# Softmax statistics of the head groups in token order over DRAM, and their factors broadcast by DMA

## The chip, the cores and the metric

The kernel runs on one core of a Trainium2 chip. The engines named here are TensorE (PE, its weight loads PEld), VectorE (DVE), ScalarE (ACT), GpSimd (POOL) and SyncE (SP), whose queue issues nearly all of the kernel's DMAs. The metric is the device time of one execution in microseconds (us), median of several runs.

## The reference

One step of a hybrid decoder layer for a prompt of 1024 tokens and 8 sampled tokens (1032 columns), model width 1024, all in fp32. What matters for the change is the attention branch:

- 3 head groups of 4 heads of 64, with windows and dilations (128, 1), (512, 4) and (2048, 16). Every token attends to itself and 128 earlier tokens at its group's dilation; each group gives an output `o` and a log-sum-exp `lse` for each token and head.
- The groups are combined per head slot:

```
w = softmax(stack(lses, axis=0), axis=0)
out[b,t,h,d] = sum over g of w[g,b,t,h] * o[g,b,t,h,d]
```

- The result (4 x 64 wide) goes through `w_attn_out`. Beside it stands a convolution branch (GLU, causal depthwise convolution of width 31, LayerNorm over the 1024 channels, swish, a projection). Both are weighted by sigmoid gates, summed and projected; then come a SwiGLU FFN and a gated per-layer embedding.

The kernel keeps for each group, token and head the negated maximum of the scores (`nm`) and the sum of exponentials (`l`). With m the smallest `nm` over the groups, a group's factor is f = exp(-(nm - m)) / sum over groups of exp(-(nm - m)) * l, and the combined output is the sum of f * o over the groups, `o` not yet divided.

## The kernel before

Activations lie with channels on the partitions and tokens along the free dimension, in three chunks of 384, 384 and 264 columns (`CH`). Every fp32 product is made of three matmuls of rounded halves (`mm3`, L256 to L258: high by high, high weight by low input, low weight by high input). A weight of 128 outputs is loaded as `raw` (512 KB) and split into `wh` by ScalarE and `wl` by VectorE. L116 is the helper through which every VectorE, ScalarE, GpSimd and SyncE instruction is recorded, so these are told apart by the names of their tiles.

The program runs in stages. Up to about 480 us it makes the convolution's input and the q, k, v projections, with the attention in units (class `Unit`) put between their banks. Then come the gate GEMMs: 8 weights into `d_gB` and 8 into `d_gA`, each over the three chunks. A chunk of one weight is a *bank*: 8 times `mm3`, 24 matmuls into one PSUM bank. The three banks of a weight are called a round here. At the end of a bank ScalarE makes the sigmoid `sg`, SyncE stores it, and `pump` lets the background work in `bg` issue a little (2.95 us by the planner's own count). The background is a list of generators, taken in order; each `yield` hands back. In this stage it holds the rest of the convolution and the sample tokens' attention, then `combine()` and then `layer_norm()`. After the gates comes the phase of `w_attn_out` on `oh` and `ol` (called the A phase here), whose first matmul is `g<-oh`, then the convolution's projection, the output projection, the FFN and the embedding.

The order of the instructions on an engine is settled when the program is built, by a scheduler that works on that issue order. Each engine then executes its own queue in that order: a waiting instruction holds all behind it, and SP's queue holds all DMAs behind a store that waits for its sigmoid.

`combine()` begins with the statistics in `NMs[g]` and `Ls[g]`, [128, 32] with a group's own order of query rows on the partitions. Masks (`mk`) and 16-row matmuls (L857) bring the first group, transposes (L861) the other two, to tiles `st` of 16 x 256, rows (head, token mod 4). There VectorE and ScalarE make the factors (`cM`, `Dn`); they are split into a high and a low part (`fx`, `fl`, the latter moved beside the former by a DMA). For each head pair `hp` the three groups' outputs come from DRAM as `ogl` (512 KB each), and L909 multiplies a constant selection matrix `sel` by `fx`, which spreads the factors over the partitions: 24 matmuls into PSUM. VectorE multiplies `ogl` by them and adds up the groups, in pieces of 128 x 512 whose tokens lie 4 apart (steps of 16 bytes): 12 multiplies and 8 additions. The result is split into `oh` and `ol`.

`layer_norm()` centres each chunk (`centre`: the mean by L1079 from `ysum`, then for each of 8 channel tiles `y - m` on VectorE, its square on ScalarE and a running sum `acc` on VectorE; L304 transposes the sum) and then scales it (`scale`: L316 spreads the reciprocal root, and each channel tile takes two scalar_tensor_tensor operations on VectorE and a sigmoid on ScalarE).

Of the kernel before, what the change touches and what calls it, by code (L numbers as in the profile page):

```python
# [41 lines left out]
CLASSIC = 3  # L42
NPG = 4
# [11 lines left out]
def decoder_step(ctx: ExitStack, tc: tile.TileContext, ins, outs):  # L55
# [87 lines left out]
    d_o = scratch("d_o", (3, 2, P, S))  # L143
    d_row = scratch("d_row", (4, SLOT))
# [15 lines left out]
    NMs = [const.tile([P, 32], F32, name=f"nm{g}") for g in range(3)]  # L160
    Ls = [const.tile([P, 32], F32, name=f"l{g}") for g in range(3)]
    osm = const.tile([P, 2, NS], F32, name="osm")
    cc = const.tile([P, 44], F32, name="cc")
# [400 lines left out]
    def stat_col(g, blk, head):  # L564
        if g == 0:
            return blk * 4 + head
        if g == 1:
            return (blk % 2) * 16 + head * 4 + blk // 2
        return (blk // 4) * 16 + head * 4 + blk % 4

    class Unit:
# [19 lines left out]
        def qk(self):  # L591
# [11 lines left out]
            for i, half in enumerate(self.halves):  # L603
                self.e[i] = e = sc("E")
                for blk in half:
                    o, nk = cols[blk]
                    for h in range(2):
                        head = hp * 2 + h
                        col = stat_col(g, blk, head)
                        if g < 2:  # L610
                            bv = biases[g][:, (head + 1) * 256 - nk:(head + 1) * 256]
                        else:
# [4 lines left out]
                                               scale=-1.0, scalar=3e38, accum_out=NMs[g][:, col:col + 1])  # L617
                        A.activation(ev, ev, AF.Exp, scale=-1.0, bias=NMs[g][:, col:col + 1],
                                     accum_out=Ls[g][:, col:col + 1])
# [16 lines left out]
        def pv(self):  # L636
# [20 lines left out]
            if self.last:  # L657
                SY.dma_start(d_o[g, self.hp], oT[:, :S])

# [92 lines left out]
    def sample_attention():  # L752
# [75 lines left out]
        selbt = cc[:, 36:44]  # L828
        for hp in range(2):
            TE.matmul(ps[:, hp * 8:hp * 8 + 8], acc[:, hp * P:(hp + 1) * P], selbt, start=True, stop=True)  # L830
            TE.matmul(ps[:, 16 + hp * 8:24 + hp * 8], acc[:, 512 + hp * P:512 + (hp + 1) * P], selbt,
                      start=True, stop=True)
# [5 lines left out]
    def combine():  # L838

        self32 = act("sel32")  # L840
        G.memset(self32[:, :1024], 0.0)
        for o in (0, 32):
            SY.dma_start(self32[o:o + 16, :1024], ins["sel16"])
        sel = act("sel", F32R)
        A.activation(sel[:, :1024], self32[:, :1024], AF.Copy)
        stt = []
        for which, src in ((0, NMs), (1, Ls)):
            per = []
            for g in range(3):
                ps = misc()  # L850
                if g == 0:
                    mk = sc("mk")
                    mkv = mk[:, :128].rearrange("p (a r) -> p a r", r=4)
                    V.tensor_mul(mkv, src[0].rearrange("p (a o) -> p a o", o=1).to_broadcast([P, 32, 4]),
                                 cc[:, 0:4].rearrange("p (o r) -> p o r", o=1).to_broadcast([P, 32, 4]))
                    for blk in range(8):
                        TE.matmul(ps[:16, blk * 32:(blk + 1) * 32], mk[:, blk * 16:(blk + 1) * 16], cc[:, 4:36],  # L857
                                  start=True, stop=True)
                else:
                    for e in range(2):  # L860
                        TE.transpose(ps[:16, e * P:(e + 1) * P], src[g][:, e * 16:(e + 1) * 16], ident)  # L861
                d = sc("st", (16, 256))
                if g < 2:
                    V.tensor_copy(d, ps[:16, :256])
                else:
                    V.tensor_copy(d.rearrange("p (l a) -> p l a", a=4),
                                  ps[:16, :256].rearrange("p (a l) -> p l a", a=4))
                per.append(d)
                yield
# [687 lines left out]
def _constants():  # L1557
# [10 lines left out]
    for hp in range(2):  # L1568
        for r in range(4):
            for f in range(P):  # L1570
                sel[(hp * 2 + f // 64) * 4 + r, hp * 4 + r, f] = 1.0
# [70 lines left out]
```

## Time and profile before

| | |
|---|---|
| time, median of 3 runs (range) | 1711.09 us (1710.15 to 1711.93) |
| profiled execution: its own time; its span | 1711.9 us; 1710.1 us |
| TensorE busy in the span | 1687.7 us (99%) |
| VectorE busy in the span | 1217.9 us (71%) |
| ScalarE; GpSimd busy | 618.0 us; 23.0 us |
| mean DMA traffic | 100 GB/s |
| convolution done on VectorE, `ysum` complete | about 555.2 us |
| first matmul of combine (L857) | 562.87 us |
| L909 matmuls | 583.0 to 601.7 us |
| first matmul of the A phase | 670.97 us |

Times of instructions are microseconds from the start of the span. A group's row gives the line, the engine, the operation, output and inputs with their shapes, the count, the busy time with the mean duration in ns, and then the idle time of the engine just before, with what ended it. An operation's record includes its pipeline's drain, so the next one on the same engine starts before it ends: a count of pace goes from start to start. Ends of matmuls are modelled.

### The profile page before, as it was taken

The page shows a single profiled execution, that of the slowest core. Times are in us where ns is not written, and L with a number is a line of the kernel's source. Part 1 is how long each engine was busy: PE and PEld are TensorE (multiplying, and loading weights), DVE is VectorE, ACT ScalarE, POOL GpSimd, SP SyncE. Part 2 cuts the span into 40 slices and gives each one's busy share as a digit, 9 for nine tenths or more (in the row PEclk, how much of TensorE's full clock was granted, in tenths as well). Part 3 has the DMA queues.
Part 4 walks back from the last instruction along what each step waited for, and adds up shares of the span by engine and source line. Part 5 has one row for each costly group of instructions (what it writes and reads, how often), then busy time and mean ns, then how long its engine had stood idle before and what let it go on. Part 6 is the DMA issues. An engine that isn't in the chain of part 4 may idle for free.

```text
span 1710.1 us, 29587 instructions
## 1 busy us (share of the span) xinstructions
PE 1687.7 (99%) x12062; PEld 1658.7 (97%) x12062; DVE 1217.9 (71%) x2156; ACT 618.0 (36%) x1265; POOL 23.0 (1%) x31
## 2 busy tenths in 40 slices
PE   7999999999999999999999999999999999999998
PEld 7999999999999899999999999999999999999998
DVE  7899879958979597644678766766666445637863
ACT  6434435444342255113444433223323211213520
POOL 0000000000000000000000000000000000000000
PEclk9999999999999999999999999999999999999999
DMA  5241121121252324523242222232333533420411
GB/s 190 64 123 66 43 67 57 49 79 56 95 178 95 124 90 156 161 81 112 76 131 72 90 93 87 89 104 99 103 115 124 198 107 113 161 95 14 154 54 46
DMA packets 82317, 171.57 MB, mean 100 GB/s; under 512 B 11058, under 2 KB 52066, under 8 KB 81798
## 3 DMA queue, kind: packets, MB, share of 16 engines
q1 hardware_dynamic: 82182, 169.70, 30.0%
q8 instruction: 94, 1.54, 0.4%
q14 instruction: 41, 0.34, 0.1%
HBM read 133.10 MB, written 50.01 MB: 107 GB/s over the span
## 4 chain that ended last, share of the span: by engine, by line
PE 90%; DVE 6%; DMA 1%; issue 1%; ACT 1%; POOL 0%; SPq 0%; POOLq 0%; DVEq 0%; ACTq 0%
PE g L256 29%; PE g L258 28%; PE g L257 28%; DVE y L116 3%; PE O L646 1%; PE S L600 1%; DVE ogl L116 1%; PE PT L628 1%; DVE wl L116 1%; PE m L316 0%; DVE sacc L116 0%; PE m L304 0%; DMA res<-d_x 0%; DMA strow<-in_state_conv_dram 0%; DMA raw<-in_w_in_dram 0%
## 5 line engine op out<-in xcount | busy, mean ns | idle before, releaser
L256 PE MATMUL g<-hh,wh 128*128 128x384 f32 (+1 forms) x1200 | 393.5, 328 | 8.5 <-ACT wh L116 8.5
L258 PE MATMUL g<-hh,wl 128*128 128x384 f32 (+1 forms) x1200 | 385.8, 322 | 1.0 <-DVE wl L116 1.0
L257 PE MATMUL g<-hl,wh 128*128 128x384 f32 (+1 forms) x1200 | 385.2, 321 | 0.0
L116 DVE SCALAR_TENSOR_TENSOR y<-z,taps,y 128x1023 f32<-128x1023 f32 (+14 forms) x240 | 304.1, 1267 | 37.1 <-ACT y L116 31.1
L256 PEld LDWEIGHTS g<-hh,wh 128*128 128x128 f32 x1200 | 227.2, 189 | 16.0 <-ACT wh L116 8.7
L258 PEld LDWEIGHTS g<-hh,wl 128*128 128x128 f32 x1200 | 226.5, 189 | 2.4 <-DVE wl L116 2.1
L257 PEld LDWEIGHTS g<-hl,wh 128*128 128x128 f32 x1200 | 227.0, 189 | 0.5 <-DVE hl L116 0.3
L257 PE MATMUL g<-ul,wh 128*128 128x344 f32 x528 | 168.6, 320 | 0.0
L258 PE MATMUL g<-uh,wl 128*128 128x344 f32 x528 | 168.4, 320 | 0.0
L256 PE MATMUL g<-uh,wh 128*128 128x344 f32 x528 | 163.0, 320 | 0.6 <-DVE fa L116 0.6
L116 DVE TENSOR_TENSOR wl<-raw,wh 128x1024 fp32r<-128x1024 f32 x106 | 129.0, 1220 | 26.7 <-ACT wh L116 23.3
L116 DVE TENSOR_TENSOR pk<-pk,g 128x258 f32<-128x258 f32 x266 | 105.3, 420 | 52.0 <-PE g L258 36.4
L256 PE MATMUL g<-mh,wh 128*128 128x258 f32 x448 | 126.9, 285 | 0.0
L258 PE MATMUL g<-mh,wl 128*128 128x258 f32 x448 | 126.5, 283 | 0.0
L257 PE MATMUL g<-ml,wh 128*128 128x258 f32 x448 | 126.5, 283 | 0.0
L116 ACT ACTIVATE wh<-raw 128x1024 fp32r<-128x1024 f32 x106 | 110.8, 1051 | 2.8 <-PE g L257 1.1
L116 DVE TENSOR_TENSOR fa<-fa,g 128x344 f32<-128x344 f32 x96 | 47.1, 511 | 76.9 <-PE g L258 76.4
L257 PEld LDWEIGHTS g<-ul,wh 128*128 128x128 f32 x528 | 99.2, 188 | 0.3 <-DVE ul L116 0.3
L258 PEld LDWEIGHTS g<-uh,wl 128*128 128x128 f32 x528 | 99.2, 188 | 0.0
L256 PEld LDWEIGHTS g<-uh,wh 128*128 128x128 f32 x528 | 98.1, 188 | 0.9 <-DVE fa L116 0.9
L256 PE MATMUL g<-th,wbh 128*128 128x258 f32 x304 | 86.0, 283 | 0.0
L257 PE MATMUL g<-ml,wah 128*128 128x258 f32 x304 | 85.9, 283 | 0.0
(245 smaller groups left out, 3802.9 us busy)
## 6 DMA issues: line engine op xcount, KB each, us to landing
raw<-in_w_in_dram SPq DMA_DIRECT2D x50, 512.0 KB
raw<-in_w_ffn_in_dram SPq DMA_DIRECT2D x44, 512.0 KB
hr<-d_h SPq DMA_DIRECT2D x22, 516.0 KB
raw<-in_w_ffn_out_dram SPq DMA_DIRECT2D x22, 512.0 KB
d_h<-pk SPq DMA_DIRECT2D x38, 258.0 KB
out_kvs_dram<-in_cache_kv_w_dram SPq DMA_DIRECT2D x16, 510.0 KB
res<-in_xT_dram SPq DMA_DIRECT2D x8, 516.0 KB
d_x<-mo SPq DMA_DIRECT2D x32, 129.0 KB
```

What stands on the lines that cost most here:

```text
L116: ins = fn(*a, **k)
L256: TE.matmul(ps, hi_w, xh, start=first, stop=False)
L257: TE.matmul(ps, hi_w, xl, start=False, stop=False)
L258: TE.matmul(ps, lo_w, xh, start=False, stop=last)
L600: TE.matmul(sp[h][:, o:o + nk], qT[h * 64:(h + 1) * 64, blk * P:(blk + 1) * P], kT[h * 64:(h + 1) * 64, (blk + 1) * P - nk:(blk + 1) * P], ...
L628: TE.transpose(ps[:, o:o + P], e[:, o:o + P], ident)
L646: TE.matmul(ps[h * 64:(h + 1) * 64, i * P:(i + 1) * P], vtok[:, k0:k0 + 64], self.p[half][:, o:o + P], start=kb == kbs[0], stop=kb == kbs[-1])
```

## The change

- A group's statistics go into one tile `stats[g]` of [128, 8 blocks, 8], the negated maxima in columns 0 to 3 (by head) and the sums in 4 to 7. The attention's instructions write there instead of into `NMs` and `Ls`.
- After a group's last unit `stats_by_tokens` writes the tile to DRAM (`d_st`) and reads it back, with the partition as the token within a block of 128: 9 DMAs for the first group and 5 for each other, all in GpSimd's queue.
- `combine` makes the factors with tokens on the partitions: VectorE works on 128 x 32 (two minima, three differences, three products and two sums for the denominator, a reciprocal, three products), ScalarE takes three exponentials, one transpose (L886) turns 96 columns into rows, ScalarE copies them to SBUF, and they go to DRAM as `d_fac`.
- For each head pair six DMAs read a head's factors for all 1024 tokens from `d_fac` and repeat them on 64 partitions (`fb`, two loads of 256 KB for each group). VectorE multiplies the whole `ogl` by `fb` (128 x 8 x 128, tokens 8 apart, steps of 32 bytes) and adds the groups contiguously (128 x 1024): 6 multiplies and 4 additions in all.
- `combine` takes `layer_norm()` as an argument and runs some of its steps between its own (W1, W2, W3), so the LayerNorm's steps are no longer all behind it. The first `ogl` loads are issued at its start, the second ones, with their `fb`, after the first head pair's sums.
- The constants `sel16` and most of `cc` go, and two GpSimd memsets.

Line numbers move: L256, L257, L258 become L261, L262, L263; L304 becomes L309, L316 L321, L1079 L1082, L116 L119.

```diff
+W1 = 6
+W2 = 6
+W3 = 4
...
+    def stats_by_tokens(g):
+        dst, src = stats[g], d_st[g]
+        G.dma_start(src, stats[g])
         if g == 0:
-            return blk * 4 + head
...
+            for b in range(8):
+                G.dma_start(dst[b * 16:(b + 1) * 16], src[:, b].rearrange("(p b) n -> p b n", b=8))
+        elif g == 1:
+            for l in range(2):
+                for e in range(2):
+                    G.dma_start(dst[l * 64:(l + 1) * 64, e * 4:(e + 1) * 4],
+                                 src[e::2, l::2])
+        else:
+            for j in range(2):
+                for i in range(2):
+                    G.dma_start(dst[j::2, i * 4:(i + 1) * 4],
+                                 src[i * 64:(i + 1) * 64, j * 4:(j + 1) * 4])
...
-                        col = stat_col(g, blk, head)
+                        nm_, l_ = (stats[g][:, blk, k:k + 1] for k in (head, 4 + head))
...
                 SY.dma_start(d_o[g, self.hp], oT[:, :S])
+                if self.hp:
+                    stats_by_tokens(g)
...
-    def combine():
+    def combine(beside):
+        st = act("stt")
+        def load_o(hp):
+            o3 = [act("ogl") for _ in range(3)]
             for g in range(3):
...
+                SY.dma_start(o3[g][:, :S], d_o[g, hp])
+            return o3
+
+        o3 = load_o(0)
+        for _ in range(W1):
+            yield next(beside)
...
+        V.tensor_tensor(top, stats[0][:, :, :4], stats[1][:, :, :4], op=ALU.min)
+        V.tensor_tensor(top, top, stats[2][:, :, :4], op=ALU.min)
+        for g in range(3):
+            V.tensor_sub(stats[g][:, :, :4], stats[g][:, :, :4], top)
+            A.activation(stats[g][:, :, :4], stats[g][:, :, :4], AF.Exp, scale=-1.0)
+        yield
+        V.tensor_mul(den, stats[0][:, :, :4], stats[0][:, :, 4:])
+        for g in range(1, 3):
+            V.tensor_mul(tmp, stats[g][:, :, :4], stats[g][:, :, 4:])
+            V.tensor_add(den, den, tmp)
+        V.reciprocal(den, den)
+        fac = st[:, 288:384]
         for g in range(3):
-            V.tensor_mul(M[:16, 256 + g * 256:512 + g * 256], M[:16, 256 + g * 256:512 + g * 256], Dn[:, 256:512])
+            V.tensor_mul(fac[:, g * 32:(g + 1) * 32].rearrange("p (h b) -> p b h", h=4), stats[g][:, :, :4], den)
         yield
...
+        ps = misc()
+        TE.transpose(ps[:96, :P], fac, ident)
+        A.activation(st[:96, 384:384 + P], ps[:96, :P], AF.Copy)
+        for _ in range(2):
+            yield next(beside)
+        SY.dma_start(d_fac.rearrange("g h b p -> (g h b) p"), st[:96, 384:384 + P])
+        for _ in range(3):
+            yield next(beside)
+
+        def load_f(hp):
+            f3 = [act("fb") for _ in range(3)]
+            for g in range(3):
+                for h in range(2):
+                    row = d_fac[g, hp * 2 + h].rearrange("(o b) p -> o (b p)", o=1)
+                    SY.dma_start(f3[g][h * 64:(h + 1) * 64, :S], row.to_broadcast([64, S]))
+            return f3
+
+        f3 = load_f(0)
+        for _ in range(W2):
+            yield next(beside)
         for hp in range(2):
...
-            ovs = [o[:, :S].rearrange("p (l r) -> p r l", r=4) for o in o3]
...
-                        TE.matmul(ps[:, e * 256:(e + 1) * 256], sel[:, (hp * 4 + r1) * P:(hp * 4 + r1 + 1) * P],
-                                  fx[:, g * 256:(g + 1) * 256], start=True, stop=True)
...
+            ovs = [o[:, :S].rearrange("p (t b) -> p b t", b=8) for o in o3]
             for g in range(3):
+                V.tensor_mul(ovs[g], ovs[g], f3[g][:, :S].rearrange("p (b t) -> p b t", b=8))
+                yield 1.2
+                if g:
+                    V.tensor_add(o3[0][:, :S], o3[0][:, :S], o3[g][:, :S])
+                    yield 1.2
             V.tensor_copy(o3[0][:, S:T], osm[:, hp])
+            o = o3[0]
+            if hp == 0:
+                o3, f3 = load_o(1), load_f(1)
             hi, lo = act("oh", F32R), act("ol", F32R)
...
+            for _ in range(W3 if hp == 0 else 0):
+                yield next(beside)
...
+        yield from beside
...
-        bg.append(combine())
-        bg.append(layer_norm())
+        bg.append(combine(layer_norm()))
```

Three places show what this does to the queues. The first is TensorE's queue at the end of the gate bank where `ysum` is complete and where combine begins. Before (m, then a number, is a PSUM tile, g a bank's):

```order
L258 MATMUL g_5475<-hh_127,wl_5343 128x384
L857 MATMUL m_5509<-cc,mk_5510 16x32 x8
L861 MATMUL m_5522<-ident,nm_106 16x128 x2
L861 MATMUL m_5527<-ident,nm_107 16x128 x2
L256 MATMUL g_5532<-hh_113,wh_5342 128x264
```

and now, with the end of that bank and then the end of the bank after the next:

```order
L263 MATMUL g_5493<-hh_126,wl_5361 128x384
L1082 MATMUL m_5528<-ysum_2001,onesD 128x384
L261 MATMUL g_5545<-hh_112,wh_5360 128x264
...
L263 MATMUL g_5605<-hh_126,wl_5459 128x384
L886 MATMUL m_5650<-ident,stt_5521 96x128
L1082 MATMUL m_5653<-ysum_2001,onesD 128x384
L309 MATMUL m_5589<-ident,acc_5531 128x128 x3
L261 MATMUL g_5655<-hh_112,wh_5458 128x384
```

Where combine's small matmuls stood, the mean of the LayerNorm's first chunk stands now; two banks later come the factors' one transpose, the second chunk's mean, and the transposes of the first chunk's sum of squares.

The second place is VectorE's queue with the first head pair's products. Before, they follow one another:

```order
L116 TENSOR_TENSOR ogl_5640<-ogl_5640,ogl_5642 128x2x256
L116 TENSOR_TENSOR ogl_5644<-ogl_5644,m_5683 128x2x256
L116 TENSOR_TENSOR ogl_5640<-ogl_5640,ogl_5642 128x2x256
L116 TENSOR_TENSOR ogl_5640<-ogl_5640,ogl_5644 128x2x256
L116 TENSOR_TENSOR ogl_5644<-ogl_5644,m_5725 128x2x256
L116 TENSOR_TENSOR ogl_5640<-ogl_5640,ogl_5644 128x2x256
L116 TENSOR_TENSOR ol_5732<-ogl_5640,oh_5731 128x1032
L116 TENSOR_TENSOR wl_5738<-raw_5438,wh_5737 128x1024
```

and now the LayerNorm's steps (`y`, `acc`, `cs`) stand between:

```order
L119 TENSOR_TENSOR acc_5684<-acc_5684,sq_5736 128x384
L119 TENSOR_TENSOR wl_5769<-raw_5456,wh_5768 128x1024
L119 TENSOR_TENSOR acc_5684<-acc_5684,sq_5740 128x384
...
L119 TENSOR_REDUCE cs_5756<-m_5752 128x3
...
L119 SCALAR_TENSOR_TENSOR y_2584<-y_2584,vecs,m_5762 128x384
L119 TENSOR_TENSOR ogl_5523<-ogl_5523,fb_5744 128x8x128
L119 TENSOR_TENSOR ogl_5524<-ogl_5524,fb_5745 128x8x128
L119 SCALAR_TENSOR_TENSOR y_2584<-y_2584,vecs,sw_5841 128x384
L119 TENSOR_TENSOR ogl_5522<-ogl_5522,ogl_5523 128x1024
L119 TENSOR_TENSOR wl_5879<-raw_5599,wh_5878 128x1024
L119 TENSOR_TENSOR ogl_5522<-ogl_5522,ogl_5524 128x1024
```

The products no longer read PSUM, and a weight's `wl` and the LayerNorm's operations are mixed with them.

The third place is SP's queue where the factors are read. Before, the factors' low part is moved between the `ogl` loads:

```order
L116 DMA d_gA<-sg_5675 128x384
L116 DMA ogl_5640<-d_o 128x1024
L116 DMA fx_5634<-fl_5635 16x768
L116 DMA ogl_5642<-d_o 128x1024
L116 DMA ogl_5644<-d_o 128x1024
L116 DMA d_gA<-sg_5717 128x264
```

and now the factors' way over DRAM, with the gates' stores between:

```order
L119 DMA d_gA<-sg_5630 128x384
L119 DMA d_fac<-stt_5521 96x128
L119 DMA fb_5743<-d_fac 64x1024 x2
L119 DMA d_gA<-sg_5680 128x384
L119 DMA fb_5744<-d_fac 64x1024
L119 DMA d_gA<-sg_5732 128x264
L119 DMA fb_5744<-d_fac 64x1024
L119 DMA fb_5745<-d_fac 64x1024 x2
L119 DMA d_gA<-sg_5797 128x384
```

The first `ogl` loads stand further ahead; the `fb` loads alternate with stores that wait for a sigmoid each.

109 lines of the change are left out of this document (17 added, 92 removed).

## The prediction

> **What bounds the kernel now.** I read the page first: who is busy, and what the chain that ended last is made of.
>
> ```profile
> PE 1687.7 (99%) x12062; PEld 1658.7 (97%) x12062; DVE 1217.9 (71%) x2156; ACT 618.0 (36%) x1265; POOL 23.0 (1%) x31
> PE 90%; DVE 6%; DMA 1%; issue 1%; ACT 1%; POOL 0%; SPq 0%; POOLq 0%; DVEq 0%; ACTq 0%
> ```
>
> TensorE sets the end; VectorE has 6% of the chain. So two things pay: matmuls that go, and waits of TensorE that go. Waits are hard to see in "busy", since a waiting matmul's record overlaps the next one. I therefore cut the stretch of the change into rounds of the gate loop, one weight each: three banks of 24 matmuls with 384, 384 and 264 columns, 72 matmuls in all. The rows give a round's length, then PE, PEld, DVE, ACT and POOL busy with counts, the granted clock, the DMA share and GB/s.
>
> ```profile
> 531.63:543.00 11.37, 11.37 (x75) 11.37 (x74) 11.05 (x10) 2.32 (x4) 0.00 (x0) 1.00 0.21 79
> 543.00:554.32 11.32, 11.32 (x74) 11.32 (x73) 11.00 (x10) 1.38 (x3) 0.00 (x0) 1.00 0.13 48
> 554.32:567.54 13.22, 13.22 (x112) 12.65 (x111) 4.92 (x11) 4.55 (x7) 0.00 (x0) 1.00 0.11 41
> 567.54:579.16 11.62, 11.62 (x76) 11.51 (x75) 6.55 (x14) 3.40 (x5) 0.00 (x0) 1.00 0.32 98
> 579.16:595.67 16.51, 15.17 (x95) 13.38 (x93) 11.51 (x13) 3.39 (x5) 0.00 (x0) 1.00 0.48 153
> 595.67:610.73 15.06, 13.54 (x83) 12.49 (x81) 14.71 (x19) 3.78 (x7) 0.00 (x0) 1.00 0.34 124
> 610.73:623.91 13.18, 12.58 (x79) 11.90 (x79) 12.94 (x27) 8.85 (x17) 0.85 (x1) 1.00 0.25 86
> 623.91:636.04 12.13, 12.13 (x79) 12.03 (x78) 11.32 (x23) 7.32 (x14) 0.85 (x1) 1.00 0.30 94
> 636.04:648.05 12.01, 12.01 (x80) 11.97 (x79) 10.58 (x27) 6.94 (x16) 1.08 (x1) 1.00 0.37 131
> 648.05:659.71 11.66, 11.66 (x78) 11.62 (x77) 11.14 (x24) 8.06 (x16) 0.00 (x0) 1.00 0.32 109
> 659.71:670.97 11.26, 11.26 (x75) 11.26 (x73) 4.35 (x7) 2.99 (x7) 0.00 (x0) 1.00 0.49 156
> ```
>
> A quiet round takes 11.35 us (the first two rows). The nine rounds from 554.32 to 670.97, in which combine and the LayerNorm run, take 116.65 us; nine quiet ones are 102.1. The **excess is 14.5 us**, most of it in the rounds that begin at 579 and 596. It is split with the chain of waits (start, us, what):
>
> ```profile
> 562.87 0.57 PE m L857 x16
> 566.90 0.57 PE m L857 x16
> 571.99 0.22 PE m L861 x2
> 583.13 0.26 PE m L909 x2
> 583.41 3.13 DVE ogl L116 x4
> 587.32 5.05 DVE ogl L116 x5
> 595.79 1.23 DVE wl L116
> 600.40 5.97 DVE ogl L116 x6
> 610.85 1.15 DVE wl L116
> ```
>
> Two halves show. TensorE's own work: L857 is 1.14 us, L861 is 8 transposes at 0.11 = 0.9, L909 24 matmuls at 0.13 = 3.1. And TensorE held back: the chain leaves it for VectorE, whose queue is full of the strided `ogl` work, and comes back through a `wl` that stands behind it. The LayerNorm's matmuls have these counts:
>
> ```profile
> L1079 PE MATMUL m<-ysum,onesD 128*128 128x384 f32 x4 | 1.6, 484 | 0.0
> L316 PE MATMUL m<-ident,r 128*128 128x128 f32 x9 | 1.5, 277 | 0.3 <-POOL r L116 0.3
> L304 PE MATMUL m<-ident,acc 128*128 128x128 f32 x9 | 1.5, 271 | 0.0
> L1079 PE MATMUL m<-ysum,onesD 128*128 128x264 f32 x2 | 0.6, 384 | 0.0
> ```
>
> At the pace of L861 and of a gate matmul (11.35/72 = 0.16) they are 18 x 0.11 + 6 x 0.17 = 3.0 us. So 14.5 = 5.1 (combine's matmuls) + 3.0 (LayerNorm's) + **6.4 us of waiting**.
>
> **The change part by part.** *TensorE.* 5.1 us go; one transpose (L886) comes, 0.1. Net -5.0 us, straight on the bound.
>
> *Statistics over DRAM.* Each group's write and its reads (9, 5 and 5 DMAs) stand in POOL's queue; behind them POOL has only the LayerNorm's power, after 570. The last group's start once its units are done, about 480.3, and VectorE wants them between the conv's second and third multiply-adds of the row that begins at 529.30, about 531.9:
>
> ```profile
> 479.16 1.09 ACT L116 ACTIVATE oT<-O 128x512 f32<-128x512 f32 x1 [0.54 <-PE O L646]
> 529.30 24.65 DVE L116 SCALAR_TENSOR_TENSOR y<-z,taps,y 128x1012 f32<-128x1012 f32 x19
> 579.53 0.63 SPq L116 DMA_DIRECT2D fx<-fl  x1
> 582.80 1.08 PEld L909 LDWEIGHTS m<-fx,sel 128*128 128x128 f32 x8
> ```
>
> The nearest small transfer is fx<-fl, 48 KB: issued at 579.53, used at 582.80, at most 3.3 us. Five one after another are 16.5 us against 51 of cover; I cost them at nothing. Without that cover each is up to 3.3 us in front of VectorE.
>
> *VectorE's small operations* (14 of 128x32, and three exponentials) now run during the convolution, which ended at 553.95, 8.9 us before TensorE wants `ysum` at 562.87. None is as long as a 384-element operation (0.47, below): under 7 us, hidden.
>
> *The order on VectorE.* The LayerNorm's first centring starts where L857 stood, at 562.87, and not behind combine: VectorE's idle stretch (4.92 and 6.55 busy of 13.22 and 11.62) is filled with it. Six multiplies of 128x1024 in steps of 32 bytes and four contiguous additions replace 12 multiplies and 8 additions of 128x512 in steps of 16. Their price comes from starts of queued operations:
>
> ```profile
> 604.32 1.08 DVE L116 TENSOR_TENSOR ogl<-ogl,ogl 128x512 f32<-128x512 f32 x1
> 605.30 1.07 DVE L116 TENSOR_TENSOR ogl<-ogl,m 128x512 f32<-128x512 f32 x1
> 611.90 0.55 DVE L116 TENSOR_TENSOR acc<-acc,sq 128x384 f32<-128x384 f32 x1
> 612.37 0.54 DVE L116 TENSOR_TENSOR y<-y,m 128x384 f32<-128x384 f32 x1
> 622.09 1.22 DVE L116 TENSOR_TENSOR wl<-raw,wh 128x1024 fp32r<-128x1024 f32 x1
> 623.23 0.55 DVE L116 TENSOR_TENSOR acc<-acc,sq 128x384 f32<-128x384 f32 x1
> 625.62 0.61 DVE L116 SCALAR_TENSOR_TENSOR y<-y,vecs,m 128x384 f32<-128x384 f32 x1
> 626.14 0.55 DVE L116 TENSOR_TENSOR acc<-acc,sq 128x384 f32<-128x384 f32 x1
> L116 DVE TENSOR_REDUCE sacc<-skv 128x256 f32<-128x1024 f32 x4 | 8.0, 2008 | 0.0
> ```
>
> So 0.98 us for 512 strided elements, 0.47 and 0.52 for 384 (0.34 for 264), 1.14 for 1024 contiguous. A multiply of 1024 in steps of 32 bytes is not in this trace. Bounds: 1.14 (as contiguous) and 3.9 (twice the strided price, if the step counts). I take 1.93: the strided reduction of 1024 took 2.01, and two strided halves 1.96. The Trainium skill ("SBUF — State Buffer", the note on cachelines under "Door 1: The DMA port swizzle") has lines of 16 bytes and a penalty for each access that crosses to a new one; by that both steps cross at every element, the price stays, and it speaks against any gain in the multiplies. The trace agrees as far as 2.1 ns per strided element against 1.2 contiguous; no run here shows 32 bytes.
>
> With these prices I walk VectorE beside TensorE, from 562.87, to the four places where TensorE needs it in the changed order:
> 1. L309 of chunk 0: 8 centrings and 7 sums, 15 x 0.47 from 563.5, done 570.6; TensorE (0.3 mean, banks 2.9 and 4.2, L886, the next mean) arrives at 570.8.
> 2. L309 of chunk 1: from 571.1, 8 centrings, a reduction, 7 sums, one multiply, two scale steps, one `wl`: done 582.8; TensorE 583.9.
> 3. From 584.5: 12 scale steps 6.2, five multiplies 9.7, four additions 4.6, two `wl`, one `ol` 3.4, small 0.6: done 609.0; TensorE brings chunk 2's mean at 610.3.
> 4. L309 of chunk 2: from 610.6, 8 centrings and 7 sums of 264, `ol`, two `wl`, two scale steps, 9.6: done 620.2; TensorE 621.3.
>
> VectorE is ahead everywhere, by 0.2, 1.1, 1.3 and 1.1 us. That is so narrow that handoffs (ScalarE's squares between, semaphores) will cost some of it. Between none and the whole 6.4 I put 1.5 us of waiting that stays.
>
> *Transfers.* d_fac leaves at about 571.5, after L886, and lands by 573.9 to 574.8 (fx<-fl's 3.3 as the bound). Then 6 loads `fb` of 256 KB, needed in pairs at 576.8, 586.6 and 588.5. In the two rounds with `ogl` loads 153 and 124 GB/s moved, 217 in their best 10 us:
>
> ```profile
> 590.00:600.00 10.00, 9.10 (x59) 8.52 (x58) 8.83 (x10) 2.90 (x4) 0.00 (x0) 1.00 0.64 217
> ```
>
> At 217 a pair takes 2.4 us: 576.3, in time. The second six wait in SP's queue behind the sigmoid of the bank that ends at 594.5, leave at 595.1, and are needed at 598.7, 601.8 and 606.0; landing at 597.5 to 602.3 they are in time too. The stores of `d_gA` queued between them wait for nothing new. By the Trainium skill ("SBUF — State Buffer", "Door 1: The DMA port swizzle") a load of 64 partitions reaches half the ports, 196 GB/s for 1 MiB, and two such do not add up. By that rule each pair is an estimated 2.7 us and the sum some 0.5 us worse; no run here shows it.
>
> *Sum.* -5.0 - 6.4 + 1.5 = **-9.9 us**. The profiled execution's own time was 1711.9 (span 1710.1), 0.8 above the median: 1702.0 in its terms, **1701.2 us against the median of 1711.09**. Its bounds: no waiting left, 1699.7; all 6.4 left, 1706.1. Downstream I cost nothing: the next phase only starts earlier.
>
> **The rivals.**
>
> *A: only the matmuls' time comes.* VectorE's lead is lost in handoffs and the waits move to the L309 places: 1711.1 - 5.0 = 1706.1. For it: four margins of about 1 us. Against: VectorE idles 13 us of the two rounds from 554.32 to 579.16, and they are used now.
>
> *B: the multiplies cost 3.9 us.* Five more multiplies of 1.93 extra before place 3 and 4, less the 2.4 us of margin there, 7.3; at place 2 1.93 less 1.1, 0.8. Waiting is 1.5 + 8.1, the gain 1.8: 1709.3, no change. Against: the reduction's 2.01.
>
> *C, slower: the broadcast is slow.* 64 partitions read one 4 KB row; if the six loads run at 60 GB/s instead of 217, a pair takes 8.7 us. VectorE's first multiply stands ahead of the sums that TensorE waits for: 5.8 us late, 4.7 past the margin; the third pair 6.8 late, the second six 3.9 and 4.5, less 2.4. Waiting 1.5 + 4.7 + 12.8 = 19: slower by 7.6, 1718.7. It decides from about 75 GB/s, where the same sum gives back all 11.4. For it: no such load in this trace. Against: the two rounds with `ogl` loads moved 153 and 124 GB/s, other traffic included.
>
> *D: the change's gain is lost after 671.* The next phase starts 10 us earlier, and if its gate loads or its weights don't follow, the end stays at 1711. Against: both come from the same queue, whose entries are released by the same banks.
>
> **How the numbers follow.** Forecast 0.62 (1699.7 to 1704.5), A 0.16, B 0.08, C 0.08, D 0.06. A measurement here tells about 0.2%, 3.4 us, from no change: faster is the forecast and A, 0.78; the same is B and D, 0.14; slower is C, 0.08. The range takes in both bounds and A, 1 us of spread below and B's end above: 1698.0 to 1709.5.
>
> **What would show it.** Right: 24 L909 matmuls gone, L309 of chunk 0 near 571 and the phase on `oh` starting near 661 instead of 670.97; multiplies of about 2.0 us; less than 2 us of waits before L309 and `wl`. Wrong: `ogl` on VectorE waiting for a DMA of `fb` (C), multiplies of 3 us or more (B), rounds after 579 still over 13 us (A), or the start at 661 with the old end (D).

## The result, and the profile after

The changed kernel took **1702.78 us** (median of 4, 1701.47 to 1703.53) against 1711.07 for the kernel before: ratio 0.9950, 95% interval 0.9939 to 0.9962, or 8.3 us faster (6.5 to 10.4). The forecast was 1701.2, 9.9 faster. The profiled execution took 1702.59 us, its span 1700.8.

The page's row of the engines, and the rounds of the gate loop over the same part of the program as those shown of before (length, then PE, PEld, DVE, ACT and POOL busy with counts, the clock, the DMA share, GB/s):

```profile
PE 1680.7 (99%) x11999; PEld 1654.7 (97%) x11999; DVE 1207.4 (71%) x2137; ACT 615.8 (36%) x1266; POOL 31.9 (2%) x48
```

```profile
552.65:564.62 11.97, 11.97 (x77) 11.70 (x75) 4.97 (x8) 3.29 (x7) 0.00 (x0) 1.00 0.12 44
564.62:577.02 12.40, 12.40 (x80) 12.03 (x79) 9.99 (x22) 5.68 (x14) 0.87 (x1) 1.00 0.32 100
577.02:590.35 13.33, 12.17 (x81) 11.86 (x79) 13.30 (x18) 6.55 (x12) 1.09 (x1) 1.00 0.49 150
590.35:601.73 11.38, 11.38 (x75) 11.38 (x73) 9.31 (x15) 3.51 (x7) 0.00 (x0) 1.00 0.84 260
601.73:613.49 11.76, 11.76 (x76) 11.69 (x75) 11.72 (x10) 3.80 (x6) 0.00 (x0) 1.00 0.60 198
613.49:626.79 13.30, 12.19 (x80) 11.83 (x79) 13.01 (x28) 8.79 (x18) 0.85 (x1) 1.00 0.38 119
626.79:638.45 11.66, 11.66 (x78) 11.62 (x77) 10.52 (x18) 6.32 (x11) 0.00 (x0) 1.00 0.53 180
638.45:649.83 11.38, 11.38 (x74) 11.38 (x73) 4.09 (x10) 4.21 (x10) 0.00 (x0) 1.00 0.14 49
649.83:661.19 11.36, 11.36 (x75) 11.36 (x74) 0.00 (x0) 1.38 (x3) 0.00 (x0) 1.00 0.19 62
```

The nine rounds take 108.54 us, 8.1 less than before's 116.65. Over nine quiet ones (102.1) that is an excess of 6.4 us where it was 14.5. Of it the LayerNorm's matmuls and the one transpose are 3.1, as costed; so by the prediction's count **3.3 us of waiting are left, where it had 1.5**. TensorE stands idle for 2.3 of them (a round's length less its PE column), in the two rounds that begin at 577 and 613. The other 1.0 is no wait: the gate matmul behind each small group of the LayerNorm's starts a little late, eight times, in the contiguous version below as well. The waits of this stretch (who waits for whom, us, times, the longest):

```profile
DVE y L119 <- ACT sw L119: 8.4, 3, 3.3
PE m L309 <- DVE acc L119: 2.3, 2, 1.2
DVE acc L119 <- ACT sq L119: 1.6, 1, 1.6
```

TensorE waits twice, both times before L309, the second and the fourth of the four places that the prediction walked through. The chain ahead of the first of these (start, us, what):

```profile
575.18 0.53 ACT sq L119
575.72 0.57 DVE acc L119
...
577.52 0.14 DVE ogl L119
577.67 2.04 issue
579.71 0.54 DVE acc L119
...
583.37 0.48 DVE acc L119
583.85 0.04 issue
583.89 0.55 PE m L309 x3
```

VectorE stood 1.6 us until ScalarE had made a square. ScalarE was not busy before that: the next entry of its queue was the sigmoid of a gate bank, which waited for that bank's last matmul, and the LayerNorm's operations stood behind it. The same holds for the 2.1 us that VectorE waits for a sigmoid `sw` from 598.0 to 600.1:

```profile
574.37 0.49 ACT L119 ACTIVATE sg<-g 128x384 f32<-128x384 f32 x1 [4.65 <-PE g L263]
599.04 0.49 ACT L119 ACTIVATE sg<-g 128x384 f32<-128x384 f32 x1 [2.57 <-PE g L263]
```

After the square, the first multiply of `ogl` by `fb` lay ahead of the remaining sums for 2.2 us (577.52 to 579.71; the "issue" is that instruction running). All six multiplies are dearer than the 1.93 us from start to start that the sum had:

```profile
L119 DVE TENSOR_TENSOR ogl<-ogl,fb x6: 2225/2280/2325, 577.5 to 609.5; 128x1024 f32<-128x1024 f32 x6
L119 DVE TENSOR_TENSOR ogl<-ogl,ogl x4: 1204/1204/1225, 591.8 to 611.7; 128x1024 f32<-128x1024 f32 x4
```

The transfers came in time. The row of SP shows d_fac issued at 570.00 and the first broadcast load at 571.69, so the way to DRAM took 1.7 us, under the bound of 3.3; no instruction waited for `fb`. On POOL the last group's statistics were out and on their way back by 475.7, some 55 us before VectorE read them:

```profile
570.00 0.38 SPq L119 DMA_DIRECT2D d_fac<-stt  x1
571.69 1.13 SPq L119 DMA_DIRECT2D fb<-d_fac  x2
...
595.77 3.64 SPq L119 DMA_DIRECT2D fb<-d_fac  x6
```

```profile
471.52 0.56 POOL L119 DMA_DIRECT2D d_st<-st  x1 [108.73 <-ACT E L119]
473.54 2.14 POOL L119 DMA_DIRECT2D st<-d_st  x4 [1.46 <-DMA d_st<-st]
```

One part of the two traces' difference can't be put down to the change. The first L830 matmul (L846 now), ahead of all this, starts at 511.22 us where it started at 512.88. In the traces of the experiments below it starts anywhere from 511.6 to 513.7, with the old and with the new statistics alike, so the 1.7 us lie within what executions differ by. The table therefore gives, beside the medians, the time from that matmul to the first one on `oh`, in which that is left out. From there to the last matmul every kernel took 1034.2 to 1035.4 us (before 1034.5, the change 1035.3).

| kernel | median us | ratio to before, 95% interval | L830/L846 to `g<-oh`, us |
|---|---|---|---|
| before | 1711.07 | | 158.1 |
| the change | 1702.78 | 0.9950 (0.9939 to 0.9962) | 150.0 |
| the change, LayerNorm behind combine | 1706.30 | 0.9973 (0.9964 to 0.9982) | 155.0 |
| before, LayerNorm between combine's steps | 1711.50 | 1.0004 (0.9995 to 1.0013) | 158.9 |
| the change, multiplies twice | 1709.82 | 0.9993 (0.9984 to 1.0002) | 157.3 |
| the change, contiguous multiplies | 1699.97 | 0.9934 (0.9920 to 0.9948) | 148.0 |
| the change, 24 matmuls put back | 1708.16 | 0.9986 (0.9977 to 0.9995) | 155.2 |
| contiguous, 24 matmuls put back | 1704.19 | 0.9956 (0.9944 to 0.9969) | 150.8 |
| the change, broadcast loads twice | 1710.90 | 0.9999 (0.9990 to 1.0008) | 157.9 |

The kernels ran in two groups, whose own runs of before had medians of 1711.32 (the first four experiments) and 1710.83 (the last ones); ratios are to these.

The stretch holds one thing beside matmuls and waits. TensorE's granted clock is at half for 3.41 us soon after that first matmul in every trace alike. In four of the experiments' traces it is at half once more: without the new order, before with the new order, multiplies twice, and broadcast loads twice (rows as above, the clock third from the end):

```profile
594.04:600.87 6.83, 5.15 (x16) 5.15 (x17) 6.83 (x8) 0.44 (x1) 0.00 (x0) 0.50 0.25 79
622.51:625.93 3.42, 3.42 (x12) 3.42 (x13) 3.42 (x4) 0.00 (x0) 0.00 (x0) 0.50 0.31 85
631.51:638.34 6.83, 3.94 (x14) 3.94 (x15) 6.29 (x16) 3.69 (x8) 1.08 (x1) 0.50 0.41 134
618.91:625.74 6.83, 3.39 (x11) 3.39 (x12) 6.83 (x7) 0.85 (x2) 0.00 (x0) 0.50 0.57 203
```

In the first, 16 matmuls take 5.15 us, 0.32 each, where a gate matmul takes 0.16. Half of the busy time in each row, an estimated 2.6, 1.7, 2.0 and 1.7 us, is therefore lost to the clock. In each of the four TensorE stood, or had just stood, for 2.0 to 5.3 us at a time; in the other five traces of the table it stands for at most 1.8 at a time after that first stretch, and the clock stays full. That the wait brings the lower clock fits all nine traces but was not tested by itself. By the executions' mean clocks most timed runs of these kernels had it too (0.997 or 0.998, where the change's four have 0.999 or 1.0), but not six of the ten of before with the new order (0.999, their median 1710.9 us).

### The profile page after: what moved, and what is told of

Its sections match the earlier page's. It is cut to its first block, busy times and chain, and to the rows that moved or that the text cites. A ratio compares the mean times of both kernels' runs of the same rounds, so it can differ in the third digit from the quotient of the medians.

```text
span 1700.8 us, 29483 instructions
## 1 busy us (share of the span) xinstructions
PE 1680.7 (99%) x11999; PEld 1654.7 (97%) x11999; DVE 1207.4 (71%) x2137; ACT 615.8 (36%) x1266; POOL 31.9 (2%) x48
## 4 chain that ended last, share of the span: by engine, by line
PE 90%; DVE 6%; issue 2%; DMA 1%; ACT 1%; POOL 0%; POOLq 0%; SPq 0%; DVEq 0%; ACTq 0%
PE g L261 29%; PE g L263 28%; PE g L262 28%; DVE y L119 3%; PE O L661 1%; PE S L616 1%; PE PT L643 1%; DVE wl L119 1%; DVE ogl L119 1%; PE m L309 0%; DVE acc L119 0%; PE m L321 0%; DVE sacc L119 0%; DMA hr<-d_h 0%; DMA res<-in_xT_dram 0%
## 5 line engine op out<-in xcount | busy, mean ns | idle before, releaser
L261 PE MATMUL g<-hh,wh 128*128 128x384 f32 (+1 forms) x1200 | 393.4, 328 | 7.2 <-ACT wh L119 7.2
L263 PE MATMUL g<-hh,wl 128*128 128x384 f32 (+1 forms) x1200 | 385.2, 321 | 0.3 <-DVE wl L119 0.3
L262 PE MATMUL g<-hl,wh 128*128 128x384 f32 (+1 forms) x1200 | 384.6, 320 | 0.0
L119 DVE SCALAR_TENSOR_TENSOR y<-z,taps,y 128x1023 f32<-128x1023 f32 (+14 forms) x240 | 304.0, 1267 | 36.7 <-ACT y L119 31.1
L261 PEld LDWEIGHTS g<-hh,wh 128*128 128x128 f32 x1200 | 227.0, 189 | 14.4 <-ACT wh L119 7.2
L262 PEld LDWEIGHTS g<-hl,wh 128*128 128x128 f32 x1200 | 226.9, 189 | 0.5 <-DVE hl L119 0.3
L263 PEld LDWEIGHTS g<-hh,wl 128*128 128x128 f32 x1200 | 226.3, 189 | 0.8 <-DVE wl L119 0.8
L262 PE MATMUL g<-ul,wh 128*128 128x344 f32 x528 | 168.8, 320 | 0.1
L263 PE MATMUL g<-uh,wl 128*128 128x344 f32 x528 | 168.5, 320 | 0.0
L261 PE MATMUL g<-uh,wh 128*128 128x344 f32 x528 | 163.1, 321 | 0.6 <-DVE fa L119 0.6
L119 DVE TENSOR_TENSOR wl<-raw,wh 128x1024 fp32r<-128x1024 f32 x106 | 129.0, 1221 | 27.0 <-ACT wh L119 23.7
L119 DVE TENSOR_TENSOR pk<-pk,g 128x258 f32<-128x258 f32 x266 | 105.4, 421 | 52.4 <-PE g L263 36.8
L261 PE MATMUL g<-mh,wh 128*128 128x258 f32 x448 | 127.0, 285 | 0.0
L263 PE MATMUL g<-mh,wl 128*128 128x258 f32 x448 | 126.5, 283 | 0.0
L262 PE MATMUL g<-ml,wh 128*128 128x258 f32 x448 | 126.4, 282 | 0.0
L119 ACT ACTIVATE wh<-raw 128x1024 fp32r<-128x1024 f32 x106 | 110.8, 1051 | 3.0 <-PE g L262 1.1
L119 DVE TENSOR_TENSOR fa<-fa,g 128x344 f32<-128x344 f32 x96 | 47.1, 511 | 77.6 <-PE g L263 77.2
L262 PEld LDWEIGHTS g<-ul,wh 128*128 128x128 f32 x528 | 99.2, 188 | 0.4 <-DVE ul L119 0.4
L263 PEld LDWEIGHTS g<-uh,wl 128*128 128x128 f32 x528 | 99.2, 188 | 0.0
L261 PEld LDWEIGHTS g<-uh,wh 128*128 128x128 f32 x528 | 98.0, 188 | 0.9 <-DVE fa L119 0.9
L261 PE MATMUL g<-th,wbh 128*128 128x258 f32 x304 | 86.0, 283 | 0.0
L263 PE MATMUL g<-th,wbl 128*128 128x258 f32 x304 | 85.9, 283 | 0.0
```

The source lines that it names most:

```text
L119: ins = fn(*a, **k)
L261: TE.matmul(ps, hi_w, xh, start=first, stop=False)
L262: TE.matmul(ps, hi_w, xl, start=False, stop=False)
L263: TE.matmul(ps, lo_w, xh, start=False, stop=last)
```

## The experiments

Theory: 5.0 us came from TensorE's own work, some 3 us from waits that the LayerNorm's earlier start saves, and what is left of waits comes from VectorE being late at L309. The rivals are named in the expectations.

**The order taken out of the change.** W1, W2, W3 are 0, and the five other steps of the LayerNorm inside combine become two plain yields, so in the order of the program it stands wholly behind combine again.

```diff
-        for _ in range(2):
-            yield next(beside)
+        yield
         SY.dma_start(d_fac.rearrange("g h b p -> (g h b) p"), st[:96, 384:384 + P])
-        for _ in range(3):
-            yield next(beside)
+        yield
```

> The changed kernel with the LayerNorm wholly behind combine again (W1, W2, W3 and the five other steps taken out). Theory (two separate gains: 5.0 us of TensorE's work, and some 3 us of waits that the LayerNorm's earlier start saves): the second is lost, 1705 to 1707. Rival (the waits went with the matmuls into PSUM and the 16-byte pieces, and the order is worth nothing): 1702 to 1703.5.

1706.30 us: the number is as the theory had it. By the medians 4.8 us of the gain stay and 3.5 go; in the stretch of the table, which is that of one execution, 5.0 go. The waits of its trace:

```profile
DVE ogl L119 <- DMA fb<-d_fac: 16.4, 1, 16.4
PE g L261 <- ACT wh L119: 2.2, 1, 2.2
PE g L263 <- DVE wl L119: 2.0, 1, 2.0
```

With 0.5 us before L321 TensorE's waits are 4.7 us where the change has 2.3. So 2.4 of the 5.0 us are waits, and the half clock is an estimated 2.6: the cause is only in part the one that the theory named. Without the LayerNorm's steps VectorE has nothing to do until the first factors are there: it stands 16.4 us, from the end of the convolution at 555.95, and then TensorE waits for weight halves that stand behind the late work. The way over DRAM is half of that:

```profile
564.34 0.38 SPq L119 DMA_DIRECT2D d_fac<-stt  x1
```

VectorE had made the factors by 543.2, but their transpose (L886) stands at the end of a gate bank, at 563.2. They leave 8.4 us after the convolution, and the first multiply starts 8.0 us later, at 572.32. So the steps between cover the factors' wait for their place in TensorE's queue as well as the broadcast's way.

**The order put into the kernel before.** The same interleaving with the old combine: 6 steps ahead of the masks, 11 behind the split of the factors, 4 before the first `ol`.

```diff
-    def combine():
+    def combine(beside):
...
+        for _ in range(6):
+            yield next(beside)
         stt = []
...
         SY.dma_start(fx[32:48, :768].bitcast(F32), fl[:16, :768].bitcast(F32))
         yield
+        for _ in range(11):
+            yield next(beside)
...
             A.activation(hi[:, :T], o3[0][:, :T], AF.Copy)
+            for _ in range(4 if hp == 0 else 0):
+                yield next(beside)
...
+        yield from beside
```

> The kernel before with only the order changed: the LayerNorm's steps stand between combine's, 6 ahead of the masks, 11 behind the split of the factors, 4 before the first ol. Theory (the earlier start saves some 3 us of waits by itself): 1707 to 1709. Rival (with L909 and its pieces in PSUM the order gives nothing or costs, since TensorE waits for VectorE to free the PSUM tiles): 1711 or more.

1711.50 us, no change: the theory missed here and the rival holds. The order is worth nothing by itself, nor does the clock hide a gain, since the executions without the second half clock have 1710.9. The waits:

```profile
PE m L913 <- DVE ogl L116: 3.6, 1, 3.6
DVE ogl L116 <- DMA ogl<-d_o: 3.4, 1, 3.4
```

(L913 is before's L909.) The broadcast matmuls stand in TensorE's own queue and wait for VectorE to work off the `ogl` pieces in their PSUM tiles, here too. The four kernels together make a square: neither 1711.1, order alone 1711.5, the new combine alone 1706.3, both 1702.8. The 3.5 us of the order, waits and clock together, exist only once the factors no longer come through PSUM.

**The multiplies made contiguous.** The token of a block's row is taken as 128 b + p instead of 8 p + b. The first group's statistics lie that way already; the other two are written to DRAM in token order (2 and 4 DMAs) and read back by one each. The factors' rows are then in token order, and so are the multiplies.

```diff
-    d_st = scratch("d_st", (3, P, 8, 8))
+    d_st = scratch("d_st", (3, S, 8))
...
+        if g == 0:
+            return
+        if g == 1:
+            dv = d_st[1].rearrange("(n q r) e -> n q r e", n=2, r=4)
+            for n in range(2):
+                G.dma_start(dv[n], stats[1][:, n::2])
+        else:
+            dv = d_st[2].rearrange("(q j i k) e -> q j i k e", j=2, i=2, k=4)
+            for j in range(2):
+                for i in range(2):
+                    G.dma_start(dv[:, j, i], stats[2][i * 64:(i + 1) * 64, j * 4:(j + 1) * 4])
+        G.dma_start(stats[g], d_st[g].rearrange("(b p) e -> p b e", p=P))
...
-                V.tensor_mul(ovs[g], ovs[g], f3[g][:, :S].rearrange("p (b t) -> p b t", b=8))
+                V.tensor_mul(o3[g][:, :S], o3[g][:, :S], f3[g][:, :S])
```

> The changed kernel with the token order taken as 8 blocks of 128, so that the six multiplies ogl*fb run over 1024 contiguous elements; the first group's statistics then need no way over DRAM. Theory (the waits that are left, about 3.3 us, come from VectorE being late at the two L309 places, and the multiplies' 2.2 us are the largest part of it): the multiplies take 1.14 us from start to start, VectorE saves 6 x 1.06 = 6.4 us, the waits before L309 at about 582 and 621 (1.3 each) go, and the time falls by 2 to 3 us, to about 1700.3. Rival (ScalarE's handoffs set what is left: VectorE waited 1.6 us for a square and 2.1 for a sigmoid): the multiplies are cheaper, the time stays within 0.7 us of 1702.8.

1699.97 us, as the theory had it, and the fastest of all: 11.4 us faster than its runs of before, ratio 0.9934. In its trace:

```profile
L119 DVE TENSOR_TENSOR ogl<-ogl,fb x6: 1217/1220/1228, 578.2 to 607.5; 128x1024 f32<-128x1024 f32 x6
```

```profile
DVE y L119 <- ACT sw L119: 10.4, 4, 3.5
PE m L309 <- DVE acc L119: 0.5, 1, 0.5
```

The multiplies fall from 2280 to 1220 ns, the wait before L309 from 2.3 to 0.5 us, and the nine rounds to 106.55 us, so that by the prediction's count 1.4 of the 3.3 us of waiting are left. VectorE's waits for ScalarE grew from 8.4 to 10.4 us and cost nothing: the rival is out.

**The multiplies made twice.** The factors stand squared in the attention's part of the output, which is therefore not the reference's.

```diff
                 V.tensor_mul(ovs[g], ovs[g], f3[g][:, :S].rearrange("p (b t) -> p b t", b=8))
+                V.tensor_mul(ovs[g], ovs[g], f3[g][:, :S].rearrange("p (b t) -> p b t", b=8))
```

> The changed kernel with each of the six multiplies made twice (the factors then stand squared in the attention's output, which is not the reference's): 6 x 2.2 = 13.2 us more on VectorE. Theory (VectorE has no margin left at the L309 places): nearly all of it comes out as waits, 11 to 13 us slower than the changed kernel, 1714 to 1716. By the prediction's margins of 2.4 us: about 10 slower, 1713. Rival (VectorE is not what TensorE waits for): under 3 us slower.

1709.82 us, 7.0 more than the change (7.3 in the stretch of the table), below both figures of the theory. TensorE's waits are 7.6 us where they were 2.3, so 5.3 of the 7.3 are waits, and the half clock is an estimated 2.0. VectorE is what TensorE waits for, but with more room than thought:

```profile
PE m L309 <- DVE acc L119: 6.4, 2, 5.3
DVE y L119 <- ACT sw L119: 2.0, 2, 1.7
PE g L263 <- DVE wl L119: 1.2, 1, 1.2
```

Of VectorE's 13.2 us some 8 do not come out as waits of TensorE, and the second row shows where most of them went: VectorE's own waits for sigmoids fall from 8.4 to 2.0. Time that VectorE spends waiting for ScalarE is spare time too.

**TensorE's work put back.** 24 matmuls of 128x256 on a gate input, whose results nothing reads, four behind each of the six multiplies in the order of the program.

```diff
+        def spare():
+            ps = misc()
+            xh = hs[1][0]
+            for e in range(2):
+                TE.matmul(ps[:, e * 256:(e + 1) * 256], xh[:, :P], xh[:, 256:512], start=True, stop=True)
+
...
+                spare()
+                spare()
                 yield 1.2
                 if g:
```

> The changed kernel with 24 matmuls of 128x256 put back, two at each of twelve places beside the products, on operands that are ready (a gate input) and with results that nothing reads: 3.1 us of TensorE's work as L909 was, without its waits. Most stand before the third L309 place, where the changed kernel waits 1.3 us. Theory (TensorE's work and VectorE's lateness meet at the L309 places, so the longer counts, not the sum): 1.8 to 2.3 us slower than 1702.8, about 1704.9. Rival (the terms add up): 3.1 slower, 1705.9. Rival (a matmul there is free): no change.

> The same 24 matmuls in the version with contiguous multiplies, where next to no waits are left before L309 (0.5 us). Theory: all 3.1 us come out, 1703.1 against 1700.0. Rival (free): 1700.

1708.16 us, 5.4 slower than the change (5.2 in the stretch), and 1704.19, 4.2 slower than the contiguous version (2.8 in the stretch, which is what 24 matmuls at 0.12 come to; the rest lies outside it). In the second the work comes out whole, as expected. In the first every expectation missed: it costs more than its own length. Two of its waits, and the matmuls that the second one holds:

```profile
PE m L309 <- DVE acc L119: 3.0, 2, 1.8
PE m L906 <- DVE y L119: 1.4, 1, 1.4
599.76 0.50 PE L906 MATMUL m<-hh 128*128 128x256 f32 x2 [1.38 <-DVE y L119]
```

(L906 is the line of the added matmuls.) They need no data from VectorE, but they take their PSUM tiles from the buffers that the LayerNorm uses too. Those at 599.76 start when VectorE has ended the last of four operations `y<-y,vecs,m` (597.51 to 599.71), which read the reciprocal root that L321 spread into such a tile. And the wait before L309 doesn't shrink by the work put ahead of it but grows, to 3.0. The two waits, 2.1 us more than the change's, and the matmuls' own 2.9 make up 5.0 of the 5.2; the clock stays full in this trace. With contiguous multiplies, where VectorE is early, neither happens.

**The broadcast made twice.** Each load of `fb` once more ahead of it, into a tile that nothing reads.

```diff
+            x3 = [act("fx") for _ in range(3)]
...
+                    SY.dma_start(x3[g][h * 64:(h + 1) * 64, :S], row.to_broadcast([64, S]))
                     SY.dma_start(f3[g][h * 64:(h + 1) * 64, :S], row.to_broadcast([64, S]))
```

> The changed kernel with every broadcast load made twice (the first into a tile that nothing reads): 24 loads of 256 KB instead of 12, so the factors come at half the rate. Rival C of the prediction (the broadcast's rate is near what VectorE needs): 4 us slower or more. Theory (the loads have some microseconds of cover; only the first pair's second half, which now stands behind the store of a sigmoid that is ready at 577.6, comes about 3 us late): 1 to 3 us slower, 1704 to 1706. Full cover: no change.

1710.90 us: 8.1 slower, the whole gain, as rival C would have it and well past what I expected. Its waits:

```profile
DVE ogl L119 <- DMA fb<-d_fac: 5.9, 1, 5.9
PE g L263 <- DVE wl L119: 5.4, 2, 4.2
PE g L261 <- ACT wh L119: 2.4, 1, 2.4
```

It is C's mechanism: a multiply that waits for its factors holds VectorE's queue, and the weight halves behind it hold TensorE. But it does not measure the margin cleanly. Of the 7.9 us in the stretch some 5.5 are more waits of TensorE (7.8, where the change has 2.3), and the half clock is an estimated 1.7. With the added loads the scheduler also placed the LayerNorm otherwise (the third chunk's mean at 590.7 instead of 610.1), so that part of the 8.1 us may be the order's. That stays open.

**The price of a step by itself.** Behind the last work of the contiguous version are written two multiplies and an addition of 128x1024 for each of six steps, with the output and one input (in the second multiply both) in steps of 4, 8, 16, 32, 64 and 128 bytes. The scheduler mixes them into that last work.

```diff
+    for step in (1, 2, 4, 8, 16, 32):
+        a3 = [act(f"pa{step}"), act(f"pb{step}")]
+        for x in a3:
+            V.memset(x[:, :S], 1.0)
+        va, vb = (x[:, :S].rearrange("p (t b) -> p b t", b=step) for x in a3)
+        V.tensor_mul(va, va, a3[1][:, :S].rearrange("p (b t) -> p b t", b=step))
+        V.tensor_mul(va, va, vb)
+        V.tensor_add(va, va, a3[1][:, :S].rearrange("p (b t) -> p b t", b=step))
```

> The version with contiguous multiplies, and behind the kernel's last work multiplies and additions of 128x1024 on tiles of their own, whose output and one or both inputs go in steps of 4, 8, 16, 32, 64 and 128 bytes: the price of the step by itself. If each element outside a line of 16 bytes pays once: 1.14 at 4 and 8, 2.0 at 16 and 2.2 at 32 and above, for both kinds. If the step counts: twice as much at 64 as at 32. The time is longer by these operations and is not compared.

The first multiply of each step in the timeline of VectorE, in that order:

```profile
1639.86 1.22 DVE L119 TENSOR_TENSOR pa<-pa,pb 128x1024 f32<-128x1024 f32 x1
...
1647.47 1.21 DVE L119 TENSOR_TENSOR pa<-pa,pb 128x1024 f32<-128x1024 f32 x1
...
1655.45 2.02 DVE L119 TENSOR_TENSOR pa<-pa,pb 128x1024 f32<-128x1024 f32 x1
...
1665.88 2.28 DVE L119 TENSOR_TENSOR pa<-pa,pb 128x1024 f32<-128x1024 f32 x1
...
1678.05 2.02 DVE L119 TENSOR_TENSOR pa<-pa,pb 128x1024 f32<-128x1024 f32 x1
...
1686.57 2.20 DVE L119 TENSOR_TENSOR pa<-pa,pb 128x1024 f32<-128x1024 f32 x1
```

Up to 8 bytes nothing, from 16 on about 0.8 to 1.1 us more, and no growth with the step: 64 bytes take less than 32. The second multiply and the addition of each step agree with the first within 0.07 us. That is the expectation's first reading, but for 64 bytes, where it had 2.2; the second (the step counts) is out.

## Why the prediction was right, and where it was off

- *Direction, size and place.* Forecast 9.9 us faster, measured 8.3 (6.5 to 10.4). The phase on `oh` began at 661.19, "near 661"; that profile was 1.7 us ahead at L846 already, and the nine rounds themselves gave 8.1.
- *TensorE's work, -5.0.* The page has 63 matmuls fewer (12062, now 11999). For L909's share it is shown: 24 matmuls put back cost 2.8 us in the stretch where next to nothing waits (3.1 costed). That the other 2.0 us (L857 and L861) come out whole was not tested by itself. The 4.8 us that stay without the new order are no second proof: waits and the half clock stand in that sum too.
- *The term that was mis-sized: 1.5 us of waiting that stays.* It measured 3.3 by the same count, 2.3 of it TensorE standing idle. The multiply was priced from steps of 16 bytes (1.93 from start to start) and has steps of 32, which took 2.28 against 2.02 us in the probe, 2.2 from start to start in place. (At 64 bytes the probe has 2.02 again, at 128 bytes 2.20; why 32 and 128 cost more stays open.) And the four margins were counted on VectorE's operations alone; the 1.6 us at 574 that it waited for a square used up the second margin of 1.1, and the 2.1 us at 598 that it waited for a sigmoid stand in the chain that leads to the fourth place. Contiguous multiplies, which change that one price and beside it only POOL's small transfers, take the waiting to 1.4.
- *How waits are saved.* The prediction read the 4.9 us of saved waits from a walk along VectorE in the new order and did not ask what the order is worth alone. The square of four kernels says: order alone gives nothing, the new combine alone 4.8, and the rest comes only with both. In before's order experiment the matmuls stand behind PSUM tiles that VectorE holds; without the order VectorE stands 16.4 us for the factors, TensorE waits 2.4 us more, and the half clock adds an estimated 2.6.
- *Transfers at nothing.* Right: the statistics' cover was some 55 us against 51 thought, d_fac's way 1.7 us. By the Trainium skill ("SBUF — State Buffer", "Door 1: The DMA port swizzle" and "Can I just issue two DMAs to hit both halves?") the 64-partition loads would go at 196 GB/s and not add up. From 597.5 to 602.5 us of the changed kernel's trace mostly `fb` loads ran:

```profile
DMA packets 412, 1.29 MB, mean 259 GB/s; under 512 B 78, under 2 KB 107, under 8 KB 412
```

  The last count less the one before it is 305 packets of 4 KB, the size of an `fb` row: 1.25 MB in 5 us, 250 GB/s. (The `ogl` loads, whose packets are as large, had all of theirs by then: 384 of them between 591.4 and 597.5.) The trace does not agree with the 196 GB/s: these loads, three to each half of the partitions, moved more together, and the measured figure decides. The 217 GB/s of the sum was a little low; it did not matter, since no instruction waited.
- *A, only the matmuls' time:* its number, 1706.1, is what the change without its order took (1706.3), by luck, since that sum holds other waits and the half clock. A part of its mechanism is in the result: the waits that are left stand before L309, and two rounds took 13.33 and 13.30 us, over the 13 that the prediction gave as A's sign; and the 2.3 us before L309 are more than the "less than 2" that it gave as a sign of being right. *B:* its price of 3.9 is out; the probe shows no growth with the step beyond 16 bytes. That is in line with the note on lines of 16 bytes in the Trainium skill ("SBUF — State Buffer", "Door 1: The DMA port swizzle"), by which each access that crosses to a new line pays. B's arithmetic turned 11.6 us of VectorE into 8.1; twice the multiplies turned 13.2 into 5.3 of waits, 7.0 with the clock. *C:* not met. With twice the loads VectorE's queue gives the gain away once the factors come late, but how far the change was from that was not measured. *D:* out, since the time after 661 is the same in all traces within 1.2 us.

## What to carry to other kernels

Work that leaves the bounding engine counts in full where no wait stands beside it (2.8 us of 2.9 here). Waits had several parties: the new way of the data and the filler that covers its latency were worth 4.8 us and nothing alone, and 8.3 together. Look at the granted clock of the stretch before a difference is called waiting: in four traces here an estimated 1.7 to 2.6 us of it was the clock. When a broadcast goes over DRAM, put other work of its consumer between, and choose the layout so that the consumer reads contiguous lines: here the second step, a different token order, gave another third of the gain. VectorE's room was larger than its margins at the four places, because its waits for ScalarE filled up too when it got more to do.

## What the runs showed of the hardware

- A VectorE multiply of 128x1024 in fp32 takes 1.22 us with elements of the output and one input 4 or 8 bytes apart, 2.02 at 16, 2.28 at 32, 2.02 at 64 and 2.20 at 128 bytes.
- Matmuls that need nothing from another engine can still wait for it, through the PSUM tiles that it has not read: 24 of them, 2.9 us of work, cost 5.2 us in the stretch of the table beside a late VectorE, 1.4 of it such a wait, and 2.8 beside an early one.
- TensorE's granted clock was at half for 3.41 or 6.83 us in the four traces in which TensorE had stood for 2.0 us or more at a time in the gate rounds, and at full there in the five with no wait over 1.8 us.
- Six 64-partition broadcast loads from DRAM moved 250 GB/s together; the three 128-partition `ogl` loads just before them moved 368 (359 packets of 4 KB from 593 to 597 us).
- A 64-partition broadcast load took 0.44 to 0.59 us to issue on SP, where the 128-partition `ogl` loads took 0.38 to 0.42.
